# Spreading the tokens' scales: later behind the sums, and as two fp32r passes on split scales in place of fp32

## The chip, the cores and the metric

The kernel runs on one core of one Trainium2 chip. The metric is the device time of one execution in microseconds; a time below is the median of several executions of the same program.

## The reference, cut to what matters

A trunk of four decoder layers works on 256 tokens of 1024 features. A layer is a SwiGLU feed-forward block (hidden size 2816), a token mixer, a second SwiGLU block, and a sigmoid gate on a per-layer embedding. The mixer of layers 0 and 3 is HGRN2, a gated linear recurrence; that of layer 1 is mLSTM; that of layer 2 is attention over a sliding window (SWA). All is float32.

```
h = x + 1/2 * SwiGLU_1(RMSNorm(x))
h = h + Mixer(RMSNorm(h))
h = h + 1/2 * SwiGLU_2(RMSNorm(h))
x = h + sigmoid(RMSNorm(h) W_gate) * (p W_ple)

RMSNorm(x) = x * rsqrt(mean(x*x over the 1024 features) + 1e-6) * gain
```

So there are four RMSNorms in a layer and sixteen in all. Each needs, per token, one sum over the features and one scale made from it.

## The kernel before, in words

**Layout.** The activations lie transposed: features on the 128 partitions, tokens along the row. The four tiles `h[0..3]` hold 1024 features x 256 tokens. All weights stream from memory in 1 MB transfers of two units (a unit is 128 x 1024 numbers). Every float32 operand of the large products is split into two fp32r parts: ScalarE (ACT) casts to the high part (L246), VectorE (DVE) subtracts to get the low part (L247). A product is then three fp32r matmuls, or, in `mm_t`, two: the high weight with both parts of x side by side (512 columns, L278) and the low weight with the high part (256 columns, L279). One such pair is called a tile here. A unit feeds eight tiles, and three units are made ahead of the one in use (`AHEAD_UNITS`).

**The norm.** A product does not wait for the norm's scale: x carries only the gain, and the scale of each token is applied to the result. `end_norm` therefore queues the making of the scale as background work (`later`), and the products tick it along: each tile adds 0.125 to a credit, and when the credit is positive the next step of the first generator in the queue is emitted, and what it yields is taken off. The steps of a norm are four squares (each weighs `W_SQ` = 1.0, eight tiles), then a pause `W_SS`, then the two matmuls with a column of ones (L402), which leave the sums per token on the partitions, the factor and the epsilon on DVE (L376), the power -0.5 on GpSimd (POOL, L377) which gives `rc` (128 tokens x 2), a pause `W_RC` = 0.5 (four tiles), then two matmuls that spread the scales over all partitions (L407: `rc` broadcast as the stationary operand, the identity as the moving one, 128 columns each), and a copy from PSUM on ACT to `rb` (L409). `rc` is used where tokens lie on the partitions, `rb` where features do.

**Who needs them.** In the feed-forward blocks `rb` scales the gates (L428), first when the eighth column tile is done, and later the output (L465). In HGRN2 it scales f and q (L660), and in the PLE gate the products (L520), followed by a sigmoid, two more DVE operations, and the push of the next layer's x (`push`, L250 and L251), which the first tiles of the next layer's feed-forward block read. SWA uses `rc` alone.

**What sets the order.** The code emits in the order told above; the framework then lays the instructions of each engine out itself, by the order in the code and by when it expects the operands to be there, adds the waits, and each engine runs its list strictly in that order. TensorE (PE) is the one on which all norms and products meet.

The constants are made in `setup`, among them `ident` by POOL.

Of the kernel before, what the change touches and what calls it, by code (L numbers as in the profile page):

```python
# [11 lines left out]
F32R = mybir.dt.float32r  # L12
# [6 lines left out]
P = 128  # L19
D = 1024  # L20
T = 256
NT = T // P
# [5 lines left out]
EPS = 1e-6  # L28
U = 1024
AHEAD_UNITS = 3  # L30
W_SQ, W_SS, W_RC = 1.0, 0.5, 0.5
ML_RATE = 1
SW_RATE = 2.5
FQ_RATE = 0.75
# [85 lines left out]
class Kern:  # L120
# [219 lines left out]
    def setup(self):  # L340
        nc, c, a = self.nc, self.const, self.a
        self.h = [c.tile([P, 512], F32, tag=f"h{j}", name=f"h{j}") for j in range(4)]
        self.gains = c.tile([P, DEPTH * N_GAIN * KT], F32, name="gains")
        nc.scalar.dma_start(out=self.gains, in_=a["gains"])
        ncol = a["cols"].shape[1]
        self.cols = c.tile([P, ncol], F32, name="cols")
        nc.scalar.dma_start(out=self.cols, in_=a["cols"])
        self.ident = c.tile([P, P], F32, name="ident")
        make_identity(nc, self.ident)
        self.ones = c.tile([P, 1], F32, name="ones")  # L350
        nc.gpsimd.memset(self.ones, 1.0)
        self.mhalf = c.tile([P, 16], F32, name="mhalf")
        nc.gpsimd.memset(self.mhalf, -0.5)
# [22 lines left out]
        nc.vector.tensor_scalar(out=out, in0=src, scalar1=1.0 / n, scalar2=EPS, op0=ALU.mult, op1=ALU.add)  # L376
        nc.gpsimd.tensor_tensor(out=out, in0=out, in1=self.mhalf[:, :w], op=ALU.pow)  # L377

    def end_norm(self):


        rc = self.small([P, NT], "rc", 2)
        rb = self.small([P, T], "rb", 2)
        return self.x, rc, rb, self.later(self.norm_steps(rc, rb))

    def norm_steps(self, rc, rb):
        nc = self.nc
        ss = self.small([P, T], "ss", 2)
        for j in range(4):
            sq = self.s512("sq")  # L390
            nc.scalar.activation(sq, self.h[j], AF.Square)
            for i in range(2):
                s = sq[:, i * T:(i + 1) * T]
                if i:
                    nc.vector.tensor_tensor(out=ss, in0=ss if j else sq[:, :T], in1=s, op=ALU.add)
                elif j:
                    nc.vector.tensor_tensor(out=ss, in0=ss, in1=s, op=ALU.add)
            yield W_SQ
        yield W_SS
        ps = self.misc()  # L400
        for t in range(NT):
            nc.tensor.matmul(ps[:, t:t + 1], ss[:, t * P:(t + 1) * P], self.ones, start=True, stop=True)  # L402
        self.rsqrt_mean(rc, ps[:, :NT], D, NT)
        yield W_RC
        pb = self.misc()
        for t in range(NT):
            nc.tensor.matmul(pb[:, t * P:(t + 1) * P], rc[:, t:t + 1].broadcast_to([P, P]), self.ident,  # L407
                             start=True, stop=True)
        nc.scalar.copy(out=rb, in_=pb[:, :T])  # L409

    @staticmethod
# [598 lines left out]
    def swa(self, l):  # L1010
        nc = self.nc
        j = l // 3
        x, rc, rb, norm = self.end_norm()
        nc.sync.dma_start(out=self.sinks, in_=self.a["sinks"][j:j + 1, :].broadcast_to([P, SW_H]))
        o = self.col_of["sw_q_norm"] + j
        nc.vector.tensor_scalar(out=self.qg, in0=self.cols[:, o:o + 1], scalar1=SW_D ** -0.5, scalar2=None,
# [239 lines left out]
```

## Time and profile before

| | |
|---|---|
| median of 3 runs | 2122.43 us (2111.08 to 2124.21) |
| the profiled execution | 2116.65 us |
| its span in the trace | 2114.9 us |
| PE busy | 2084.7 us (99%), 12261 matmuls |
| DVE busy | 1540.0 us (73%) |
| ACT busy | 1204.6 us (57%) |
| POOL busy | 52.9 us (2%) |
[...]

The profile is of one execution. Its time is 5.8 us under the median of the three runs and within their spread. Busy shares count an engine's instructions; matmul ends are modelled, so idle gaps of PE are best read from the starts of neighbouring matmuls.

### The profile page before, as it was taken

The page shows a single profiled execution, that of the slowest core. Times are in us where ns is not written, and L with a number is a line of the kernel's source. Part 1 is how long each engine was busy: PE and PEld are TensorE (multiplying, and loading weights), DVE is VectorE, ACT ScalarE, POOL GpSimd, SP SyncE. Part 2 cuts the span into 40 slices and gives each one's busy share as a digit, 9 for nine tenths or more (in the row PEclk, how much of TensorE's full clock was granted, in tenths as well). Part 3 has the DMA queues.
Part 4 walks back from the last instruction along what each step waited for, and adds up shares of the span by engine and source line. Part 5 has one row for each costly group of instructions (what it writes and reads, how often), then busy time and mean ns, then how long its engine had stood idle before and what let it go on. Part 6 is the DMA issues. An engine that isn't in the chain of part 4 may idle for free.

```text
span 2114.9 us, 30560 instructions
## 1 busy us (share of the span) xinstructions
PE 2084.7 (99%) x12261; PEld 1822.4 (86%) x12261; DVE 1540.0 (73%) x2063; ACT 1204.6 (57%) x1678; POOL 52.9 (2%) x84
## 2 busy tenths in 40 slices
PE   8999999999999999999999999999999999999998
PEld 7888889888888888888888887788888888898887
DVE  7766987775877576776687667677687768967766
ACT  7555656554755466655565547655466545565544
POOL 1000000000000000000000001000000000000000
PEclk9999999999999999999999999999999999999999
DMA  7555344555455544555545552355545553445551
GB/s 283 199 187 181 118 160 166 198 191 188 171 190 194 183 160 161 183 182 197 184 176 198 181 198 101 118 182 190 188 169 197 192 191 128 143 177 186 192 187 73
DMA packets 53855, 372.26 MB, mean 176 GB/s; under 512 B 6352, under 2 KB 6992, under 8 KB 9424
## 3 DMA queue, kind: packets, MB, share of 16 engines
q1 hardware_dynamic: 53424, 370.21, 48.5%
q8 instruction: 96, 1.57, 0.3%
q14 instruction: 47, 0.39, 0.1%
q10 hardware_dynamic: 288, 0.09, 0.0%
HBM read 369.23 MB, written 1.05 MB: 175 GB/s over the span
## 4 chain that ended last, share of the span: by engine, by line
PE 91%; DVE 5%; issue 2%; ACT 1%; POOL 1%; DMA 0%; ACTq 0%; DVEq 0%; POOLq 0%
PE acc L278 50%; PE acc L279 26%; PE acc L268 2%; PE acc L260 2%; PE acc L270 2%; PE acc L269 2%; PE acc L259 2%; PE acc L261 2%; PE mis L694 1%; DVE wl L247 1%; DVE slab L701 1%; DVE slab L707 1%; PE mis L1077 1%; POOL rc L377 0%; PE mis L407 0%
## 5 line engine op out<-in xcount | busy, mean ns | idle before, releaser
L278 PE MATMUL acc<-x,wh 128*128 128x512 f32 x3392 | 1188.3, 395 | 8.7 <-DVE x L251 7.2
L247 DVE TENSOR_TENSOR wl<-wraw,wh 128x1024 fp32r<-128x1024 f32 (+1 forms) x693 | 844.5, 1222 | 474.6 <-ACT wh L246 470.6
L246 ACT CAST wh<-wraw 128x1024 fp32r<-128x1024 f32 (+1 forms) x693 | 726.4, 1050 | 750.7 <-PE acc L278 433.4
L279 PE MATMUL acc<-x,wl 128*128 128x256 f32 x3392 | 950.5, 280 | 0.0
L278 PEld LDWEIGHTS acc<-x,wh 128*128 128x128 f32 x3392 | 636.3, 188 | 154.9 <-DVE x L251 8.9
L279 PEld LDWEIGHTS acc<-x,wl 128*128 128x128 f32 x3392 | 640.8, 189 | 0.0
L278 PE MATMUL acc<-slab,wh 128*128 128x512 f32 x1152 | 403.8, 394 | 0.0
L279 PE MATMUL acc<-slab,wl 128*128 128x256 f32 x1152 | 321.9, 279 | 0.0
L278 PEld LDWEIGHTS acc<-slab,wh 128*128 128x128 f32 x1152 | 215.8, 187 | 49.7
L279 PEld LDWEIGHTS acc<-slab,wl 128*128 128x128 f32 x1152 | 217.3, 189 | 0.0
L303 DVE TENSOR_TENSOR gu<-acc,gu 128x512 f32<-128x512 f32 x176 | 120.3, 683 | 6.9 <-ACT gu L302 6.6
L302 ACT COPY gu<-acc 128x512 f32<-128x512 f32 x176 | 101.9, 579 | 14.5 <-PE acc L279 14.5
L268 PE MATMUL acc<-wh,x 128*128 128x512 f32 (+1 forms) x272 | 102.6, 379 | 0.0
L269 PE MATMUL acc<-wl,x 128*128 128x512 f32 (+1 forms) x272 | 100.4, 369 | 0.0
L270 PE MATMUL acc<-wh,x 128*128 128x512 f32 (+1 forms) x272 | 100.1, 368 | 0.0
L278 PE MATMUL acc<-wide,wh 128*128 128x512 f32 x256 | 91.7, 394 | 0.0
L259 PE MATMUL acc<-slab,wh 128*128 128x256 f32 x256 | 74.1, 291 | 0.1
L260 PE MATMUL acc<-slab,wh 128*128 128x256 f32 x256 | 72.9, 285 | 0.0
L261 PE MATMUL acc<-slab,wl 128*128 128x256 f32 x256 | 72.6, 284 | 0.0
L279 PE MATMUL acc<-wide,wl 128*128 128x256 f32 x256 | 71.5, 279 | 0.0
L250 ACT ACTIVATE x<-h,gains 128x256 fp32r<-128x256 f32 x128 | 57.4, 501 | 21.6 <-DVE h L466 19.8
L430 DVE TENSOR_TENSOR gu<-gu,gu 128x512 f32<-128x512 f32 x88 | 60.8, 691 | 5.8 <-ACT gu L429 2.9
(236 smaller groups left out, 1777.0 us busy)
## 6 DMA issues: line engine op xcount, KB each, us to landing
wraw<-in_w_all SPq DMA_DIRECT2D x346, 1024.0 KB, 4.8
wraw<-in_w_all SPq DMA_DIRECT2D x7, 512.0 KB, 8.3
pt<-in_pT SPq DMA_DIRECT2D x4, 256.0 KB, 3.9
h<-in_xT SPq DMA_DIRECT2D x3, 256.0 KB, 5.1
outT<-h SPq DMA_DIRECT2D x3, 256.0 KB, 2.0
wraw<-in_w_all SPq DMA_DIRECT2D x2, 256.0 KB, 4.5
h<-in_xT SPq DMA_DIRECT2D x2, 128.0 KB, 4.4
outT<-h SPq DMA_DIRECT2D x2, 128.0 KB, 1.7
```

Of the source, the lines that this page charges most:

```text
L246: self.nc.scalar.copy(out=hi, in_=src)
L247: self.nc.vector.tensor_tensor(out=lo, in0=src, in1=hi.bitcast(F32), op=ALU.subtract)
L259: mm(ps, wh[:, cs], xh, start=first and opens, stop=False, skip_group_check=True)
L260: mm(ps, wh[:, cs], xl, start=False, stop=False, skip_group_check=True)
L261: mm(ps, wl[:, cs], xh, start=False, stop=last, skip_group_check=True)
L268: mm(ps, xh[:, ts], wh[:, cs], start=first, stop=False, skip_group_check=True)
L269: mm(ps, xh[:, ts], wl[:, cs], start=False, stop=False, skip_group_check=True)
L270: mm(ps, xl[:, ts], wh[:, cs], start=False, stop=last, skip_group_check=True)
L278: mm(ps, wh[:, cs], x, start=first, stop=False, skip_group_check=True)
L279: mm(ps[:, T:], wl[:, cs], x[:, :T], start=False, stop=last, skip_group_check=True)
L302: nc.scalar.copy(out=o3, in_=p4[:, :, 1, :])
L303: nc.vector.tensor_tensor(out=o3, in0=p4[:, :, 0, :], in1=o3, op=ALU.add)
```

## The change

The pause between the sums and the spreading grows from 0.5 to 1.25 (from four tiles to ten), except in SWA, where it stays 0.5. Right after the power, `rc` is split into an fp32r high and low part, as the weights are: a cast on ACT and a subtraction on DVE, 128 x 2 each. The spreading then takes, per half of the tokens, two fp32r matmuls that add up in PSUM, with an fp32r copy of the identity, in place of one fp32 matmul. The copy of the identity is made once at the start, on ACT.

```diff
-W_SQ, W_SS, W_RC = 1.0, 0.5, 0.5
+W_SQ, W_SS, W_RC, W_RC_SW = 1.0, 0.5, 1.25, 0.5
...
         make_identity(nc, self.ident)
+        self.ident_r = c.tile([P, P], F32R, name="ident_r")
+        nc.scalar.copy(out=self.ident_r, in_=self.ident)
...
-    def norm_steps(self, rc, rb):
+    def norm_steps(self, rc, rb, w_rc):
...
         self.rsqrt_mean(rc, ps[:, :NT], D, NT)
-        yield W_RC
+        rh, rl = (self.small([P, NT], n, 2, F32R) for n in ("rch", "rcl"))
+        self.split(rh, rl, rc)
+        yield w_rc
         pb = self.misc()
         for t in range(NT):
-            nc.tensor.matmul(pb[:, t * P:(t + 1) * P], rc[:, t:t + 1].broadcast_to([P, P]), self.ident,
-                             start=True, stop=True)
+            for i, r in enumerate((rh, rl)):
+                nc.tensor.matmul(pb[:, t * P:(t + 1) * P], r[:, t:t + 1].broadcast_to([P, P]), self.ident_r,
+                                 start=i == 0, stop=i == 1)
         nc.scalar.copy(out=rb, in_=pb[:, :T])
...
-        x, rc, rb, norm = self.end_norm()
+        x, rc, rb, norm = self.end_norm(W_RC_SW)
```

## Rows read from the trace of the kernel before

**Rows 1.** The page: busy time by engine (us, share, instructions); the chain by engine.

```profile
PE 2084.7 (99%) x12261; PEld 1822.4 (86%) x12261; DVE 1540.0 (73%) x2063; ACT 1204.6 (57%) x1678; POOL 52.9 (2%) x84
...
PE 91%; DVE 5%; issue 2%; ACT 1%; POOL 1%; DMA 0%; ACTq 0%; DVEq 0%; POOLq 0%
```

**Rows 2.** Waits of PE, then of ACT: total us, times, longest us.

```profile
PE mis L407 <- POOL rc L377: 3.8, 4, 1.1
...
ACT wh L246 <- PE acc L278: 433.4, 319, 3.5
```

**Rows 3.** Line L407 and its SWA case in time (start, us, instruction).

```profile
L407 PE MATMUL mis<-ident,rc x64: 270/275/377, 40.3 to 2099.3; 128*128 128x128 f32 x64
...
1265.57 0.28 PE L269 MATMUL acc<-wl,x 128*128 128x256 f32 x1
1265.69 0.28 PE L270 MATMUL acc<-wh,x 128*128 128x256 f32 x1
1265.81 0.60 PE L407 MATMUL mis<-ident,rc 128*128 128x128 f32 x4
1266.17 0.36 PE L268 MATMUL acc<-wh,x 128*128 128x256 f32 x1
```

**Rows 4.** PE in time around L402 of the same norm.

```profile
1263.83 0.28 PE L270 MATMUL acc<-wh,x 128*128 128x256 f32 x1
...
1264.31 0.36 PE L268 MATMUL acc<-wh,x 128*128 128x256 f32 x1
```

**Rows 5.** PE in time around L407, PLE of layer 0.

```profile
545.99 0.39 PE L278 MATMUL acc<-x,wh 128*128 128x512 f32 x1
...
546.89 0.37 PE L279 MATMUL acc<-x,wl 128*128 128x256 f32 x1
```

**Rows 6.** PE in time around L407, mLSTM norm.

```profile
758.20 0.28 PE L279 MATMUL acc<-x,wl 128*128 128x256 f32 x1
...
759.46 0.48 PE L278 MATMUL acc<-x,wh 128*128 128x512 f32 x1
```

**Rows 7.** PE in time, first norm of layer 1.

```profile
570.05 0.50 PE L402 MATMUL mis<-ones,ss 128*128 128x1 f32 x4
...
571.21 0.27 PE L279 MATMUL acc<-x,wl 128*128 128x256 f32 x1
572.56 0.71 PE L407 MATMUL mis<-ident,rc 128*128 128x128 f32 x4 [1.08 <-POOL rc L377]
573.03 0.48 PE L278 MATMUL acc<-x,wh 128*128 128x512 f32 x1
```

**Rows 8.** Line L278 between 547.05 and 570.04 us, weight loads (ns min/median/max).

```profile
L278 PEld LDWEIGHTS acc<-x,wh x66: 186/187/192, 547.0 to 569.7; 128*128 128x128 f32 x66
```

**Rows 9.** The tile rc: DVE and POOL (ns min/median/max).

```profile
L376 DVE TENSOR_SCALAR rc<-mis x16: 147/151/160, 39.2 to 2097.7; 128x2 f32<-128x2 f32 x16
L377 POOL TENSOR_TENSOR rc<-rc,mhalf x16: 695/698/1608, 39.5 to 2098.0; 128x2 f32<-128x2 f32 x16
```

**Rows 10.** ACT in time at the start.

```profile
4.76 0.62 ACT L246 CAST wh<-wraw 128x512 fp32r<-128x512 f32 x1 [1.75 <-DMA wraw<-in_w_all]
...
8.85 0.21 ACT L600 ACTIVATE lb_e<-lb_e 128x32 f32<-128x32 f32 x1
```

**Rows 11.** HGRN2 of layer 0: DVE and ACT after rb.

```profile
213.19 1.22 DVE L660 TENSOR_TENSOR slab<-slab,rb 128x1024 f32<-128x1024 f32 x1
...
215.97 1.28 ACT L661 ACT_TABLE_LOAD   x1
```

**Rows 12.** PLE of layer 0: ACT's rb, DVE's first push.

```profile
547.17 0.37 ACT L409 COPY rb<-mis 128x256 f32<-128x256 f32 x1 [0.36 <-PE mis L407]
...
553.58 0.88 DVE L251 SCALAR_TENSOR_TENSOR x<-h,gains,x 128x256 fp32r<-128x256 f32 x2 [0.36 <-ACT x L250]
```

**Rows 13.** The end: DVE on the last column tile.

```profile
2109.87 0.42 DVE L303 TENSOR_TENSOR gs<-acc,gs 128x256 f32<-128x256 f32 x1 [1.30 <-ACT gs L302]
```

**Rows 14.** ACT in time, SWA norm: what waits for POOL.

```profile
1265.52 0.84 ACT L999 ACTIVATE sq<-acc,rc 128x256 f32<-128x256 f32 x2 [2.43 <-POOL rc L377]
```

More of the change, by code (lines that the diff above doesn't have):

```diff
@@ L377, in rsqrt_mean, with end_norm @@
         nc.gpsimd.tensor_tensor(out=out, in0=out, in1=self.mhalf[:, :w], op=ALU.pow)
-    def end_norm(self):
+    def end_norm(self, w_rc=W_RC):
         rc = self.small([P, NT], "rc", 2)
         rb = self.small([P, T], "rb", 2)
-        return self.x, rc, rb, self.later(self.norm_steps(rc, rb))
-    def norm_steps(self, rc, rb):
+        return self.x, rc, rb, self.later(self.norm_steps(rc, rb, w_rc))
+    def norm_steps(self, rc, rb, w_rc):
         nc = self.nc
```

## The prediction, made before the result was known

> **What bounds the kernel.** I read the page first: PE is busy 99% of the span and the chain that ended last runs on PE for 91% [rows 1]. The time is therefore the sum of what PE executes plus the few places where it stands, and anything on DVE, ACT or POOL counts only where PE waits for it. The list of PE's waits comes next. The scale's power on POOL is named there for 3.8 us in 4 waits [rows 2]; a wait is counted only from the modelled end of the matmul before, so I read the true price from start to start, in PE's timeline around each of the sixteen L407 groups.
>
> **What a norm's spreading costs PE now.** In SWA the group waits for nothing. From L270 to the next L268 it is 0.48 us, where undisturbed neighbours lie 0.12 apart: the four passes of the two fp32 products insert 0.36 us [rows 3]. That is the bare price; the last PLE (0.37) and the first block (0.45) repeat it. Elsewhere a wait comes on top. Between L278 and its L279, normally 0.23 apart, lie 0.90 us in PLE 0: 0.67 inserted [rows 5]; the other two such PLEs cost the same, and the two HGRN2 norms and four second feed-forward norms 0.55 to 0.60 (3.46 together). The mLSTM norm costs 1.26 - 0.12 = 1.14 [rows 6]. The first norms of layers 1 to 3 cost 1.82 - 0.12 = 1.70 each, 5.12 together [rows 7]. Sum: 1.18 + 3 x 0.67 + 3.46 + 1.14 + 5.12 = 12.9 us, of which 16 x 0.37 = 5.9 is the bare insertion and 7.0 is waiting for `rc`. So 7.0 us, 0.33% of the time, is all that a later place can return.
>
> **Part 1, the later place.** Six tiles more are 6 x 0.35 = 2.1 us of other PE work, where `rc` now comes 0.1 to 0.8 us late. In the eleven norms where the wait is 0.8 or less it goes: 7.0 - 3 x 1.34 = 3.0 us. The three first norms of layers 1 to 3 are different. There L402 already runs late, because the squares of the last pushed h come late: after PLE 0's L407, which lies in tile 42 of 64, PE starts 66 tiles before L402 [rows 8], so L402 stands behind tile 44, not behind tile 37 where its step falls due. L407 follows only two and a half tiles on [rows 7], fewer than the four of the old pause. Its place is set by when the framework expects the scale, and a due time of tile 47 changes that place by half a tile at most. The real delay is POOL's: its power takes 0.70 us at the median and 1.61 in four cases, these three and mLSTM [rows 9]. I count nothing for these three; if all of it went, it would be 4.0 us more. **-3.0 us, bounds -7.0 and 0.**
>
> **Part 2, the passes.** Four passes stay four: an fp32 product is two passes now (64 records for 32 products), and an fp32r product pair is two. No row shows an fp32r pass of 128 columns. From below: fp32r passes of 256 columns start 0.12 apart [rows 3]; half of that is 0.058, four are 0.23, 0.13 less than now, 2.1 us in sixteen norms. From above: an fp32r pass could take what a whole fp32 product of 128 columns takes, twice 0.108 (L407's four passes span 0.60, each lasts 0.275 [rows 3]); four are 0.86, 0.50 more, 8.0 us. I take no change, because the nearest row says that columns do not set the price: L402, with one moving column, inserts the same 0.36 us as L407 with 128 [rows 4], so what is left is the weight load of each pass, and there are still four (an fp32r load lasts 187 ns [rows 8]). **0, bounds -2.1 and +8.0.**
>
> [...]
>
> **Part 3, the split.** Per norm one ACT cast, at most the 0.21 us of a 128x32 operation [rows 10], and one DVE subtraction like L376, 0.15 us [rows 9]; 16 x 0.36 us off PE's path, under the six tiles of cover. SWA keeps the old pause, and its L407 came just as `rc` was there: +0.4 us. In the three uncovered norms the scale is later by 0.36 too, but the framework can move the place with it: 0 (bounds 0 and 3 x 1.6, if the subtraction also stands behind a 1.2 us weight subtraction). The copy of the identity falls into ACT's 1.75 us of waiting for the first weights [rows 10]: 0; uncovered it would be about 0.3 us. **+0.4 us, up to +5.2.**
>
> **Part 4, a later `rb`.** No DMA moves. `rb` lands about 1.6 us later (from the middle of tile 42 to behind tile 47). The gates of the feed-forward blocks need it at tile 64, so nothing there. Three places are close. HGRN2: L660 ends at 214.41 and ACT's next step begins at 215.97 [rows 11], 1.56 us of slack for 1.6 of delay; behind it is a chain that PE does wait for. I take 0.3 for each of the two layers, at most 1.6 each. PLE into the next layer: the first half of the first push ends at about 554.0 [rows 12] and PE asks for it at 546.89 + 22.5 x 0.35 = 554.7, so 0.7 us of slack; of the 6.5 us from `rb` to that push about 1.9 are other work that can go first. I take 0.4 us for each of three layers, at most 1.3 each. The end: DVE stood 1.30 us before the last column tile [rows 13], against 2.1 us of delay there: +0.4, at most 0.8. **+2.2 us, bounds 0 and +7.9.**
>
> **Sum.** -3.0 + 0 + 0.4 + 2.2 = -0.4 us. On the profiled execution of 2116.65 us this is 2116.2; that execution lies 5.8 us under the median of 2122.43, on which it would be 2122. The four executions shown average 2118.6, so I forecast **2118 us: no difference that a measurement can tell** (about 1% is the least that it can for this kernel).
>
> **Rivals.**
> - *The waits of layers 1 to 3 go too* (22%). The due time then does decide there. For it: the new due tile is 47, the place now is 46 to 47. Against: L407 is spaced by readiness. Another -4.0: 2114; with part 4 hidden, 2112.
> - *The passes cost their columns only* (8%): -2.1, 2116. Against it stands L402's row.
> - *An fp32r pass of 128 columns costs as much as an fp32 product* (18%). Its place is L407 itself; +8.0, so 2126, slower than before. It decides as soon as a pass inserts 0.1 us, since the net gain is only 0.4 us. For it: no row shows a fast one this narrow. Against: the columns do not set the price now.
> - *The queues stand* (4%). The cast waits on ACT for POOL, the subtraction on DVE for the cast, and behind them stand the weights' casts and subtractions; PE waits for the weights. That such a wait holds the rest is in the trace: ACT stood 2.43 us at L999 for `rc` [rows 14]. Price: POOL's 14.8 us plus 16 x 0.36 = 20.6 us if nothing covers it, 2139, and 2159 with a 1.2 us subtraction in front each time. It decides where fewer than about 2 us of weights lie ahead. Against: ACT's casts wait 433 us for PE to free a buffer [rows 2], so weights are ready ahead nearly everywhere.
> - *The change does not move L407* (6%): the framework keeps it where the scale is expected. 2118 to 2119.
>
> [...]
>
> **Chances.** The forecast has 42%. Every case but the queues lies between 2112 and 2126. The runs of before lie 7.5 us under and 5.6 over their mean, so I widen to 2107 to 2129. Over 1% faster (under 2101) would need more than all waits and all insertions together, 12.9 us: 2%, for scatter alone. Over 1% slower (over 2143) is most of the queue case: 4%. Within 1%: 94%.
>
> **What would show it.** Right: no PE wait for POOL at L407 outside the first norms of layers 1 to 3, where a wait of about 1 us stays, now for DVE's low part; an insertion near 0.37 us in the other norms; L407's place behind ten tiles after L402; small new waits of PE for x (L251) at the start of layers 1 to 3. Wrong: passes starting 0.06 or 0.2 us apart; waits for `wl` on PE; the three waits of layers 1 to 3 gone.

## The result: 1% slower

| | before | after |
|---|---|---|
| median (4 runs each) | 2118.86 us (2111.08 to 2124.21) | 2145.32 us (2132.91 to 2148.14) |
| ratio, 95% interval | | 1.0105 (1.0081 to 1.0129) |
| profiled execution, span | 2114.9 us | 2143.6 us |

The forecast was 2118 us, the range 2107 to 2129: the time lies outside it, on the slower side. Nothing in the changed kernel's totals says why. The page's busy times and its chain by engine are nearly those of [rows 1]:

```profile
PE 2108.2 (98%) x12261; PEld 1836.1 (86%) x12261; DVE 1543.0 (72%) x2079; ACT 1208.2 (56%) x1695; POOL 51.9 (2%) x84
...
PE 92%; DVE 5%; ACT 1%; issue 1%; POOL 0%; DMA 0%; SPq 0%; DVEq 0%; ACTq 0%; POOLq 0%
```

PE's number of instructions is the same, and it is busy 23.5 us longer: much of the loss is no wait at all, but the same matmuls taking longer. The waits of PE, answering to [rows 2], give the other part (total us, times, longest us):

```profile
PE acc L278 <- DVE x L251: 16.2, 4, 7.7
PE mis L699 <- DVE slab L706: 4.0, 4, 1.1
PE acc L278 <- DVE gs L303: 3.4, 1, 3.4
PE mis L1054 <- ACT kd L1045: 2.5, 1, 2.5
```

The waits for `rc` are gone. In their place PE waits for the pushed x: one of the four is the start (7.2 us before, 7.7 here), the other three are 2.8 us each, at the first tile of layers 1, 2 and 3. The wait for `gs` at the end was 1.4 us before.

**The spreading itself.** In SWA, answering to [rows 3] (PE in time):

```profile
1274.94 0.28 PE L270 MATMUL acc<-wh,x 128*128 128x256 f32 x1
1275.06 0.28 PE L412 MATMUL mis<-ident_r,rch 128*128 128x128 f32 x1
1275.20 0.33 PE L412 MATMUL mis<-ident_r,rcl 128*128 128x128 f32 x1
1275.37 0.27 PE L412 MATMUL mis<-ident_r,rch 128*128 128x128 f32 x1
...
1275.59 0.33 PE L268 MATMUL acc<-wh,x 128*128 128x256 f32 x1
```

From L270 to L268 it is 0.65 us, so 0.53 inserted where the fp32 passes inserted 0.36. The first norm of layer 1, answering to [rows 7]:

```profile
577.29 0.28 PE L279 MATMUL acc<-x,wl 128*128 128x256 f32 x1
577.41 0.22 PE L412 MATMUL mis<-ident_r,rch 128*128 128x128 f32 x1
577.47 0.28 PE L412 MATMUL mis<-ident_r,rcl 128*128 128x128 f32 x1
...
577.80 0.45 PE L278 MATMUL acc<-x,wh 128*128 128x512 f32 x1
```

From L279 to L278 it is 0.51 us: 0.51 - 0.12 = 0.39 inserted, against 1.70 before. The first two passes start 0.06 us apart here. Over the sixteen norms the insertion fell from 12.9 to 7.4 us. The tile `rc` and the split, answering to [rows 9] (ns min/median/max):

```profile
L378 DVE TENSOR_SCALAR rc<-mis x16: 149/150/161, 41.1 to 2123.0; 128x2 f32<-128x2 f32 x16
L379 POOL TENSOR_TENSOR rc<-rc,mhalf x16: 697/698/1544, 41.3 to 2123.3; 128x2 f32<-128x2 f32 x16
L246 ACT CAST rch<-rc x16: 185/190/193, 42.0 to 2124.1; 128x2 fp32r<-128x2 f32 x16
L247 DVE TENSOR_TENSOR rcl<-rc,rch x16: 152/155/163, 42.3 to 2124.3; 128x2 fp32r<-128x2 f32 x16
```

**The PLE of layer 0.** ACT from `rb` on, then DVE, answering to [rows 12]:

```profile
550.15 0.37 ACT L414 COPY rb<-mis 128x256 f32<-128x256 f32 x1 [1.88 <-PE mis L412]
550.49 1.05 ACT L246 CAST wh<-wraw 128x1024 fp32r<-128x1024 f32 x1
551.44 0.58 ACT L302 COPY gs<-acc 128x512 f32<-128x512 f32 x1
552.04 1.28 ACT L526 ACT_TABLE_LOAD   x1
```

```profile
550.56 1.29 DVE L525 TENSOR_TENSOR gs<-gs,rb 128x512 f32<-128x512 f32 x2 [1.05 <-ACT rb L414]
551.77 1.22 DVE L247 TENSOR_TENSOR wl<-wraw,wh 128x1024 fp32r<-128x1024 f32 x1
552.90 0.68 DVE L303 TENSOR_TENSOR gs<-acc,gs 128x512 f32<-128x512 f32 x1
553.62 0.69 DVE L525 TENSOR_TENSOR gs<-gs,rb 128x512 f32<-128x512 f32 x1
554.23 1.28 DVE L527 TENSOR_TENSOR gs<-gs,pw 128x512 f32<-128x512 f32 x2
555.44 1.28 DVE L528 TENSOR_TENSOR h<-gs,h 128x512 f32<-128x512 f32 x2
...
558.38 1.66 DVE L251 SCALAR_TENSOR_TENSOR x<-h,gains,x 128x256 fp32r<-128x256 f32 x4
```

Before, ACT loaded the sigmoid's table directly behind `rb` (at 547.56, 1.28 us long), and DVE took the first two products (L522) and sums one tile after the other. Now a weight's cast and the next column tile's copy come ahead of the table, and on DVE the first two tiles go side by side: their gates, a weight's subtraction, both products, both sums, the third tile's product, another weight's subtraction, and only then their pushes. From the start of `rb` to the first push it was 6.41 us and is 8.23. PE then, and the windows around it (start:end, length; busy us and instructions of PE, its weight loads, DVE, ACT and POOL; then the granted clock, 1.00 being full speed (on the mean of the span it is 1.000 before and 0.992 here); then the DMA share and GB/s):

```profile
555.88 0.28 PE L279 MATMUL acc<-x,wl 128*128 128x256 f32 x1
559.00 0.47 PE L278 MATMUL acc<-x,wh 128*128 128x512 f32 x1 [2.84 <-DVE x L251]
...
560.92 0.63 PE L278 MATMUL acc<-x,wh 128*128 128x512 f32 x1
561.35 0.41 PE L279 MATMUL acc<-x,wl 128*128 128x256 f32 x1
561.56 0.63 PE L278 MATMUL acc<-x,wh 128*128 128x512 f32 x1
```

```profile
550.00:555.50 5.50, 5.50 (x33) 4.79 (x32) 4.91 (x8) 5.32 (x8) 0.00 (x0) 1.00 0.33 97
560.00:563.00 3.00, 3.00 (x11) 2.54 (x10) 3.00 (x8) 1.74 (x4) 0.00 (x0) 0.50 0.00 0
```

The wait is followed by about five tiles at 0.64 us in place of 0.35: the granted clock is 0.50. That is 1.5 us more, so each of the three waits costs about 4.3 us in this execution. The end repeats it. DVE takes three tiles' products and two sums ahead of a fold that frees PSUM for PE, and its stand before the last column tile, 1.30 us in [rows 13], is 2.84. PE in time:

```profile
2133.53 0.79 PE L278 MATMUL acc<-x,wh 128*128 128x512 f32 x1 [3.38 <-DVE gs L303]
2134.12 0.41 PE L279 MATMUL acc<-x,wl 128*128 128x256 f32 x1
2134.33 0.63 PE L278 MATMUL acc<-x,wh 128*128 128x512 f32 x1
```

That is 2.0 us more of waiting than before and four tiles at half clock (0.50 from 2134 to 2136 us), 1.2 us.

**The tiles.** The last part shows only in counts. These are the matmuls of L278 alone in 160 us of the first layer's second feed-forward block (window, length, busy us and count of the matmuls, then of their weight loads, then clock and DMA), in the kernel before and then in a second execution of the changed kernel (e6 below).

```profile
380.00:540.00 160.00, 160.00 (x463) 86.56 (x462) 1.00 0.53 190
```

```profile
380.00:540.00 160.00, 160.00 (x454) 85.12 (x453) 1.00 0.52 186
```

160 us / 463 is 346 ns a tile, 160 / 454 is 352 (the tiles cut at the window's ends count as whole), at full clock in both and with no wait between. In every profile the long stretches, from one norm to the next, run at one of two spacings, 347 or 353 ns from tile to tile. A slow stretch of a second feed-forward block (some 500 tiles) costs 3 us.

**The account** of 28.7 us between the two spans: three waits for x 8.5; tiles at half clock 6.4 (22 more); the start's wait 0.5; the end's 2.0; SWA 6.4, nearly all of it a lower clock in this execution (0.76 and 0.83 in two windows of 20 us; 0.8 us in the second execution); the mean tile 350.8 in place of 348.4 ns over 4,700 tiles 11.2; the spreading -5.5. Sum 29.5, 0.8 too many.

### The profile page after: what moved, and what is told of

It reads as the page before. It is cut to its first block, busy times and chain, and to the rows that moved or that the text cites. A ratio compares the mean times of both kernels' runs of the same rounds, so it can differ in the third digit from the quotient of the medians.

```text
span 2143.6 us, 30618 instructions
## 1 busy us (share of the span) xinstructions
PE 2108.2 (98%) x12261; PEld 1836.1 (86%) x12261; DVE 1543.0 (72%) x2079; ACT 1208.2 (56%) x1695; POOL 51.9 (2%) x84
## 4 chain that ended last, share of the span: by engine, by line
PE 92%; DVE 5%; ACT 1%; issue 1%; POOL 0%; DMA 0%; SPq 0%; DVEq 0%; ACTq 0%; POOLq 0%
PE acc L278 51%; PE acc L279 26%; PE acc L268 2%; PE acc L270 2%; PE acc L269 2%; PE acc L260 2%; PE acc L261 2%; PE acc L259 2%; PE mis L699 1%; DVE wl L247 1%; PE mis L1082 1%; DVE slab L706 1%; DVE slab L712 1%; PE mis L687 0%; DVE gs L527 0%
## 5 line engine op out<-in xcount | busy, mean ns | idle before, releaser
L278 PE MATMUL acc<-x,wh 128*128 128x512 f32 x3392 | 1203.7, 399 | 19.7 <-DVE x L251 16.2
L279 PE MATMUL acc<-x,wl 128*128 128x256 f32 x3392 | 953.7, 281 | 0.0
L278 PEld LDWEIGHTS acc<-x,wh 128*128 128x128 f32 x3392 | 641.2, 189 | 174.3 <-issue 9.4
L279 PEld LDWEIGHTS acc<-x,wl 128*128 128x128 f32 x3392 | 644.3, 190 | 0.0
L278 PE MATMUL acc<-slab,wh 128*128 128x512 f32 x1152 | 406.7, 396 | 0.0
L279 PE MATMUL acc<-slab,wl 128*128 128x256 f32 x1152 | 322.3, 280 | 0.0
L278 PEld LDWEIGHTS acc<-slab,wh 128*128 128x128 f32 x1152 | 216.2, 188 | 52.1
L279 PEld LDWEIGHTS acc<-slab,wl 128*128 128x128 f32 x1152 | 217.3, 189 | 0.0
L268 PE MATMUL acc<-wh,x 128*128 128x512 f32 (+1 forms) x272 | 103.4, 383 | 0.0
L270 PE MATMUL acc<-wh,x 128*128 128x512 f32 (+1 forms) x272 | 101.2, 372 | 0.0
L278 PE MATMUL acc<-wide,wh 128*128 128x512 f32 x256 | 92.4, 396 | 0.0
L279 PE MATMUL acc<-wide,wl 128*128 128x256 f32 x256 | 71.6, 280 | 0.0
L433 DVE TENSOR_TENSOR gu<-gu,rb 128x512 f32<-128x512 f32 x88 | 60.7, 692 | 8.0 <-ACT rb L414 5.4
```

What stands on the lines that cost most here:

```text
L268: mm(ps, xh[:, ts], wh[:, cs], start=first, stop=False, skip_group_check=True)
L270: mm(ps, xl[:, ts], wh[:, cs], start=False, stop=last, skip_group_check=True)
L278: mm(ps, wh[:, cs], x, start=first, stop=False, skip_group_check=True)
L279: mm(ps[:, T:], wl[:, cs], x[:, :T], start=False, stop=last, skip_group_check=True)
```

## The experiments

Ratios are to the kernel before on the same chip, with their 95% interval. "Stretches" are the four behind the spreadings of the second feed-forward blocks.

**e1, the pause alone.** `W_RC` 1.25 (SWA 0.5), the rest as before.

> Kernel before with the longer pause alone (fp32 passes, no split; SWA keeps 0.5). Theory A (the later rb in the PLE norms makes the next layer's first x late; PE stands 2.8 us three times and 3.4 us at the end, and its clock falls to half for about 3 us after each): those four waits are here too, 12 us and 6 to 7 us of half clock, less the 6 to 7 us of waits for rc that go: 2128 to 2133 against 2119 for before. Theory B (the split and the fp32r passes cost the time): none of the four waits, 2112 to 2114.

1.0033 (1.0019 to 1.0048). The three waits are there (2.9 us each), without split or fp32r passes, but the ratio is a third of the loss: theory A explains the waits and not the time.

**e2, the split with the old pause.** The changed kernel with `W_RC` = 0.5.

> Changed kernel with the old pause of 0.5 everywhere (split and fp32r passes alone). Theory A: the four waits for x and gs are gone; the waits for the scale at the spreading grow by about 0.4 us per norm; SWA's wait for kd and its half clock (6 to 8 us in the changed kernel) may stay: 2122 to 2132. Theory B: as slow as the changed kernel, 2140 to 2146.

1.0069 (1.0057 to 1.0081), and the three waits of 2.8 us are there too: here `rb` is late because the low part stands behind a weight's subtraction on DVE. So not the pause, but a later `rb` by any cause brings the wait.

**e3, the old pause in the PLE alone.** In `ple`: `self.end_norm(W_RC_SW)`.

> Changed kernel with the pause of 0.5 in the PLE norms as well as in SWA. Theory A: the four waits and the half clock behind them go, 17 to 19 us: 2124 to 2130, the rest being SWA's. Theory B: 2140 to 2146.

1.0077 (1.0062 to 1.0092); the waits stay, for the reason of e2; the wait at the end falls to 1.4 us.

**e4, the longer pause outside the PLE.** e1 with 0.5 in `ple` too.

> Kernel before with the longer pause alone, and that neither in the PLE norms nor in SWA. Theory A: no new wait, and the waits for rc in the first norms of layers 1 to 3, the mLSTM norm and the small ones outside PLE go, 5 to 6 us: 2112 to 2115. Theory B: also 2112 to 2114; this run is the version that should beat both if A holds.

0.9995 (0.9985 to 1.0005). No wait for x. With e1 this puts the PLE's later `rb` at 0.0038, 8 us. But the waits for `rc` went outside the first norms and the PLE, and the time did not fall. The tiles' spacing may have taken it back: of the eight long stretches behind the feed-forward norms four ran at 353 ns in its profile, against two in the first profile of the kernel before and three in e5. One execution each does not show it.

**e5 and e6, both kernels again.** No edit.

> The kernel before, unchanged. In the first profile the tiles of the feed-forward blocks run at 347 or at 353 ns, a block at a time. If that is a state of the single execution (theory A), another execution has the slow spacing in other blocks and its span differs by 3 us for each block, 2114.9 +- 8 us, with no new wait. If it is set by the program (rival), the same blocks are slow again and the span is within 1 us of 2114.9.

> The changed kernel, unchanged. By both theories PE waits again 2.8 us for x at the start of layers 1 to 3 and 3.4 us for gs at the end, since the program fixes those. Open is SWA: if its lower granted clock (0.76 from 1280 to 1300 us, 0.83 from 1340 to 1360) belongs to the program, it is there again within 0.05; if it is a chance of the execution, one of the two stretches is at 0.95 or more and the span is 3 us or more under 2143.6.

e5: span 2119.1 us, the same waits; the stretch behind the last layer's first norm at 353 ns where it had 347: the spacing is not fixed by the program alone. But the four stretches had 347 again. e6: span 2142.7, the waits as they were, SWA's clock at 1.00 and 0.91 in the two windows that had 0.76 and 0.83, and SWA, from its sums to those of the next norm, 107.1 us long as against 112.7 (106.3 before); four of four stretches at 353. Most of SWA's loss was thus of that execution; the total did not fall, since more tiles were slow. (The profile of e2 has SWA at 112.9 us again.)

**e7, the split in SWA alone.**

> The kernel before, with the split and the two fp32r passes in the SWA norm alone, all pauses as before. Theory A: in SWA the split has no cover (the spreading came just as the scale was there), what follows is late and PE's clock falls there, as in the changed kernel: 2125 to 2128 us, clock under 0.9 in a stretch between 1260 and 1360 us. Rival: the split costs its own 0.4 us and SWA's loss came from what lay ahead of it: 2119 to 2121 us, clock 0.97 or more there. No wait for x at the start of a layer by either.

1.0010 (0.9998 to 1.0021): by its time theory A falls. The lowest clock, 0.91 from 1320 to 1340 us, lies between what the two expected. SWA is 0.8 us longer than before, but that is not shown to be the split's price: e14 and e18 below, without the split in SWA, have one such stretch of lower clock there too and the same length, 107.0 us. All eight profiles with the split in SWA have such a stretch and five of the twelve without, so whether the split invites it stays open.

**e8, the PLE first.** The changed kernel, in `flush` of `ple`:

```diff
-                add(j, gs, 0, 2)
-                if not last:
-                    self.push(j)
+                with self.tc.high_priority():
+                    add(j, gs, 0, 2)
+                    if not last:
+                        self.push(j)
```

> The changed kernel, with the PLE's gates and the push of x behind them put ahead in the framework's order (ACT then takes the sigmoids before the copy of the next column tile, DVE the products and sums before the third tile's and a weight's subtraction). rb is as late as in the changed kernel. Theory A (the wait of 2.8 us is the order that the later rb brings, not rb's lateness itself): the waits for x shrink from 2.8 to about 0.9 us each, the clock stays above 0.95 at the starts of layers 1 to 3, and the time is 7 to 10 us under the changed kernel's 2145: 2135 to 2138. Rival (rb's lateness itself): the waits stay at 2.5 us or more and the time at 2142 to 2147.

1.0072 (1.0052 to 1.0091), 2129.99 us: by ratio 7 us under the changed kernel, though the two intervals overlap. PE's wait at the start of layer 1, then DVE from `rb` to the push:

```profile
560.35 0.47 PE L278 MATMUL acc<-x,wh 128*128 128x512 f32 x1 [0.99 <-DVE x L251]
```

```profile
553.75 1.29 DVE L525 TENSOR_TENSOR gs<-gs,rb 128x512 f32<-128x512 f32 x2 [1.05 <-ACT rb L414]
...
559.74 0.47 DVE L251 SCALAR_TENSOR_TENSOR x<-h,gains,x 128x256 fp32r<-128x256 f32 x1
```

The wait is 1.0 us, with 1.00 as the clock behind it. `rb` (553.35) to the push is 6.39 us, as before the change: theory A holds for the waits. The sum closes: `rb` comes 7.5 us ahead of the tile that needs x before (554.7 less 547.17) and 5.85 ahead after (556.0 less 550.15), 1.7 less; the order adds 8.23 - 6.41 = 1.8; the slack was 0.7. 1.7 + 1.8 - 0.7 = 2.8, and 1.0 without the order's part.

**e9, the longer pause in the second feed-forward norms alone.** fp32 passes; `self.end_norm(W_RC_F1 if f else W_RC)`.

> The kernel before, with the longer pause in the norms of the four second feed-forward blocks alone; fp32 passes. Their four spreadings stop waiting (0.55 to 0.60 us inserted now, 0.37 then): 0.8 us less. Theory A (a short wait of PE at the spreading leaves the tiles behind it at 347 ns, none leaves them at 347 or 353): one to three of the four stretches behind these spreadings run at 353 ns in the profile, where none of twelve did in three profiles with the old pause; each costs about 3 us up to the PLE's norm, so 2 to 9 us more: 2 to 8 us over the kernel before. Rival (the spacing has nothing to do with the place): all four at 347 ns or no more slow ones than elsewhere, and the time 1 us under to 1 us over the kernel before.

1.0014 (1.0002 to 1.0026); one stretch of four at 353. A weak yes: its sign is that of theory A, and its size is hardly above the scatter.

**e10, the split and fp32r passes outside the PLE and SWA.** e4 with them.

> The changed kernel, with fp32 passes and the old pause in the PLE and SWA norms: e4 with the split and the two fp32r passes added in the other eleven norms. PLE keeps the order of the kernel before, so no wait of 2.8 us for x by either theory. Theory A (the split and the fp32r passes cost something of their own beyond the PLE, through the tiles' spacing behind the spreading): 5 to 9 us over the kernel before, at least two of the four stretches of the second feed-forward blocks at 353 ns. Rival (outside the PLE they are free): as e4, within 2 us of the kernel before.

1.0075 (1.0061 to 1.0089), more than either theory had. No wait for x, clock 0.999, and four of four stretches at 353: against e4 the difference is 0.0080, 17 us. By this pair three quarters of the loss are here, with no new wait for x to show for it.

**e11, the pause alone with the PLE first.** e1 with e8's edit.

> e1 (longer pause, fp32 passes, no split) with the PLE's gates and push put ahead in the framework's order, as in e8. Theory A (order): the three waits for x shrink from 2.8 to 0.5 us or less (rb is about 0.4 us earlier than in e8, where 1.0 was left), the clock stays full there, and 4 to 8 us of e1's 7 over the kernel before go: -1 to +3 us. The 3.3 us wait for gs at the end stays. Rival (rb's lateness itself): waits of 2 us or more stay, +5 to +8 us.

1.0039 (1.0025 to 1.0053): the waits for x shrink from 2.9 to 1.0 us and the clock stays at 1.00 there, but by ratio the time does not fall under e1's (theory A had it 4 to 8 us under). In the first norms of layers 1 to 3 PE waits for `rc` again (2.5 us in 3), and the end's wait is 3.9. The order's part is shown by the waits; what it is worth in time, this pair does not show.

**e12, the old pause in the second feed-forward norms.** The changed kernel, `self.end_norm(W_RC_SW if f else W_RC)`.

> The changed kernel, with the old pause in the norms of the four second feed-forward blocks. Theory A (the wait sets the spacing): PE waits there again for the scale's parts, 0.2 to 1 us each, and the four stretches behind run at 347 ns (in the two profiles of the changed kernel seven of eight ran at 353): 4 to 10 us under the changed kernel, 2135 to 2141 us. Rival: the waits come back and nothing else changes: 1 to 4 us over the changed kernel, 2146 to 2149. The three waits of 2.8 us for x stay by both.

(The expectation counted the slow ones wrongly: six of eight.) 1.0088 (1.0072 to 1.0103), 2133.33 us: all four stretches at 347 ns, as theory A has it. By ratio that is 0.0017, 4 us, under the changed kernel, with overlapping intervals. The three waits of 2.8 us stay.

**The place in the tile.** In these traces one thing goes with the spacing. With the old pause the spreading lies inside a tile, between L278 and its L279; with the long one mostly between two tiles. (In e2 and e12 PE takes the four fp32r passes of these norms in two places: one pass inside a tile, the other three inside a later one, behind the low part.) PE in time at the same norm (layer 1, second block), in the kernel before and then in the changed kernel:

```profile
872.43 0.40 PE L278 MATMUL acc<-x,wh 128*128 128x512 f32 x1
872.75 0.71 PE L407 MATMUL mis<-ident,rc 128*128 128x128 f32 x4
873.22 0.36 PE L279 MATMUL acc<-x,wl 128*128 128x256 f32 x1
```

```profile
877.40 0.28 PE L279 MATMUL acc<-x,wl 128*128 128x256 f32 x1
877.52 0.22 PE L412 MATMUL mis<-ident_r,rch 128*128 128x128 f32 x1
...
877.98 0.45 PE L278 MATMUL acc<-x,wh 128*128 128x512 f32 x1
```

The next four kernels tick all background work inside the tile:

```diff
         mm(ps, wh[:, cs], x, start=first, stop=False, skip_group_check=True)
+        self.tick(mid)
         mm(ps[:, T:], wl[:, cs], x[:, :T], start=False, stop=last, skip_group_check=True)
...
-            self.tick(0.125)
```

**e13, the kernel before so; e14, e4 so.**

> The kernel before, with every background step ticked between the two matmuls of a tile instead of behind the second one. Theory A (the place in the tile sets the spacing behind it): fifteen spreadings, where they fall inside a tile, leave 347 ns; the two to four stretches that run at 353 in the kernel before mostly go to 347, each 0.5 to 3 us: 1 to 6 us under the kernel before. Rival (place and spacing only go together by chance): mean spacing and time as before, within 2 us.

> e4 (longer pause outside PLE and SWA, fp32 passes) with every background step ticked inside the tile. Theory A: all four stretches of the second feed-forward blocks and both HGRN2 stretches at 347 ns (e4: one and two of them at 353): 3 to 8 us under e4's ratio of 0.9995, so 0.996 to 0.998. Rival: as e4.

e13: 0.9998 (0.9989 to 1.0006), all four at 347 as before; nothing to gain there. e14: 0.9982 (0.9973 to 0.9990), all four and both HGRN2 stretches at 347: with fp32 passes a place inside the tile goes with the fast spacing throughout (the table below), and the longer pause then returns a little.

**e15, the changed kernel so; e16, e10 so.**

> The changed kernel with every background step ticked inside the tile. Theory A: the stretches behind its spreadings go from 353 to 347 ns, 8 to 14 us under the changed kernel (ratio to before 1.004 to 1.008); the three waits of 2.8 us for x stay. Rival (the split or the passes slow the tiles wherever they lie): at least half of the stretches stay at 353 and the ratio at 1.010 or more.

> e10 (split and longer pause outside PLE and SWA) with every background step ticked inside the tile. Theory A: e10's ratio of 1.0075 falls to 1.000 +- 0.002, its four stretches of the second feed-forward blocks go from 353 to 347 ns; with e15 this closes the account: what is left of the loss is the PLE's order. Rival: 1.005 or more.

e15: 1.0112 (1.0095 to 1.0130), four of four at 353: the rival. e16: 1.0037 (1.0024 to 1.0051), two of four: between the two. So the place does not decide for fp32r passes. Behind the first norms of layers 1 to 3 of e15, whose four passes lie inside a tile too but insert 0.39 us and not 0.64, all three stretches ran at 347.

**e17, the four passes two and two.** e16 with `yield 0.125` between the halves.

> e16 with the spreading's four fp32r passes dealt over two neighbouring tiles, two inside each. Theory A (four in one place leave the slow spacing, two and two do not): the four stretches of the second feed-forward blocks and the two of HGRN2 at 347 ns, ratio 0.998 to 1.001 to the kernel before. Rival (fp32r passes leave it as chance has it, wherever they lie): one or more of the four at 353, ratio 1.003 or more.

1.0095 (1.0077 to 1.0112), four of four at 353: theory A falls. The extra step also puts off HGRN2's (PE waits 8.4 us for a slab there, 4.3 in e16).

**e18, the split made but not used.** e16 with fp32 passes on `rc`.

> e16 with the split made and not used: the spreading takes the fp32 passes on the unsplit scale. Theory A (the fp32r passes are what costs): as e14, ratio 0.997 to 0.999, stretches at 347 ns. Rival (the split's cast and subtraction are what costs): as e16, 1.003 or more.

0.9976 (0.9966 to 0.9986), 2110.39 us: theory A holds, and it is, with e14, the version that beats both kernels. The pair e18 and e16 differs in the passes alone (and so in what they wait for: `rc` or its parts). The first stretch's count and the spreading in PE's time, first of e18, then of e16:

```profile
380.00:540.00 160.00, 160.00 (x463) 86.32 (x462) 1.00 0.52 190
```

```profile
363.29 0.39 PE L278 MATMUL acc<-x,wh 128*128 128x512 f32 x1
363.51 0.61 PE L414 MATMUL mis<-ident,rc 128*128 128x128 f32 x4
363.88 0.36 PE L280 MATMUL acc<-x,wl 128*128 128x256 f32 x1
```

```profile
380.00:540.00 160.00, 160.00 (x454) 85.06 (x454) 1.00 0.51 185
```

```profile
364.82 0.39 PE L278 MATMUL acc<-x,wh 128*128 128x512 f32 x1
365.05 0.22 PE L414 MATMUL mis<-ident_r,rch 128*128 128x128 f32 x1
...
365.58 0.27 PE L414 MATMUL mis<-ident_r,rcl 128*128 128x128 f32 x1
365.69 0.33 PE L280 MATMUL acc<-x,wl 128*128 128x256 f32 x1
```

From L278 to its partner 0.59 us with fp32, 0.87 with fp32r. Between the two spans (2108.8 and 2121.1) lie 12.3 us: 2.3 in the insertions and some 10 in the tiles' mean spacing (347.7 and 349.9 ns, 4,700 tiles).

| passes and place, second feed-forward norms | kernels | stretches at 353 ns |
|---|---|---|
| fp32, inside a tile | before, e5, e7, e13, e14, e18 | 0 of 24 |
| fp32, between tiles | e1, e4, e9, e11 | 5 of 16 |
| fp32r, between tiles | after, e6, e3, e8, e10 | 14 of 20 |
| fp32r, four inside one tile | e15, e16 | 6 of 8 |
| fp32r, one inside a tile, three in a later one | e2, e12 | 0 of 8 |
| fp32r, two and two in neighbouring tiles | e17 | 4 of 4 |

The stretches behind the first norms of layers 1 to 3 in the same profiles bear the first three rows out: fp32 inside a tile 0 of 9, fp32 between tiles 8 of 21, fp32r between tiles 10 of 12. With fp32r inside they are mixed: 2 of 6 with four in one tile, 6 of 12 with one and three. So one and three is no safe place either; only behind fp32 passes inside a tile was the slow spacing never found.

## Why the prediction was wrong

By ratios, the change is the sum of: the pause outside the PLE and SWA -0.0005 (e4), the later `rb` in the PLE +0.0038 (e1 less e4), the fp32r passes +0.006 to +0.008 (e16 less e18, e10 less e4). Together 0.009 to 0.011; measured 0.0105. That this closes so well is in part luck: the parts were measured in different surroundings, and the middle one is unsure. After less e10 and e15 less e16, which both hold the PLE and SWA, give 0.0030 and 0.0075, and e11, with most of the wait gone, was no faster than e1.

- **Part 1, the waits: right in kind, larger.** -5.5 us at the spreadings against -3.0. The three first norms fell from 1.70 to 0.39, which the prediction left out and gave to a rival (22%). That rival's reason, the due time, is not borne out: without the 2.8 us wait for x (e4, e8, e10, e11) PE still waits 0.7 to 0.9 us there; with it and the long pause (after, e6, e1, e3, e12, e15) it does not. So it was most likely the new wait that gave POOL its time. And the returned time bought nothing by itself: e4 lost 3.1 us of waiting at the spreadings (12.9 to 9.8 inserted) and gained nothing.
- **Part 2, the passes: the step that failed most.** The prediction set them at 0 because four passes stay four; that the weight load of each is the price was its estimate, and no run shows it (a load's record lasts 185 to 192 ns, while the passes start 0.06 to 0.16 us apart in fifteen of the sixteen groups). The last two of each group do start 0.11 us apart, like fp32's, but the whole is not the same: 0.39 to 0.53 us inserted between tiles against 0.36, and 0.64 inside (e16). (Where 0.39 is inserted, the first two passes are 0.06 apart, which the prediction had named as a sign that it is wrong.) That is some 2 us. What the prediction had no term for is what the passes leave behind them: 353 in place of 347 ns for hundreds of tiles, 10 us. The rival "as dear as an fp32 product" had the sign and, by its +8.0, about the size, with another mechanism: it looked at L407 alone.
- **Part 3, the split: right, and smaller still.** 0.19 and 0.16 us an operation; in SWA no price of its own is shown where +0.4 was set (e7 is as long there as e14 and e18), and nothing elsewhere (e18 against e14). Only in the PLE, with the old pause, does the low part behind a 1.2 us subtraction make `rb` late (e2, e3): the prediction had that delay, but at the three first norms.
- **Part 4, the later `rb`: failed in the PLE.** The delay was foreseen (1.6 us, measured 1.7) and so was the slack (0.7). What failed is "of the 6.5 us about 1.9 are other work that can go first": the framework put more ahead, not less, and the way from `rb` to x grew by 1.8. So 2.8 us each in place of 0.4, over the bound of 1.3, and 1.5 at half clock on top, for which no term stood (e8, with the order put back, has waits of 1.0 us and the clock at 1.00). The end was mis-sized the same way: 2.0 of wait and 1.2 of clock against 0.4. HGRN2 lost nothing (its waits on L699 are 4.0 us, on L694 in e5 4.6).
- **The queues** did not stand: ACT's casts wait 9.6 us for the power on POOL, and PE never for weights. The range was too narrow because it took a cost only where an instruction is added or a wait appears.

What stays open: why fp32r passes leave the slow spacing more often than fp32 ones, why at the second feed-forward norms two and two left it behind four times of four and one and three never, and what the two spacings are.

## What to carry to other kernels

A step that is moved in the code is laid out anew by the framework: compare the order of instructions on each engine, not only the step's own time, and ask what stands between the moved result and the first matmul that needs it. PE was busy 98% of the changed kernel's span, and 11.2 us of its loss was the tiles' mean spacing, with no wait: count matmuls in equal windows before and after. A wait of PE can be dearer than it looks: here 2.84 us of it cost about 4.3, as the granted clock stood at 0.50 behind it.

## What the runs showed of the hardware

- The same pair of matmuls (512 and 256 columns) has two spacings at a granted clock of 1.00, 347 and 353 ns (463 and 454 of L278 in 160 us), and held one over hundreds of tiles, from one norm to the next: in the kernel before 347 from 400 to 540 us and, two spreadings on, 353 from 580 to 640. In a slow stretch the tiles take 350, 350 and 360 ns in turn (the first norm of layer 1 in the kernel before), in a fast one 346 or 347 each (e18, 400 to 540 us) or 343 and 350 in turn (the kernel before, 400 to 540 us).
- After a wait of 2.84 us the granted clock was 0.50 for about five tiles, beginning 0.5 to 0.9 us after PE had started again (the three waits of the changed kernel). Over seven profiles (after, e1, e2, e3, e6, e12, e15) it fell at 17 of the 21 waits of 2.7 to 2.9 us for x; after the six waits of 1.0 us in e8 and e11 it stayed at 1.00.
- Of the four fp32r passes of 128 columns in a spreading (L412 of the changed kernel, sixteen groups) the last two start 0.11 us apart throughout. The second and third start 0.11 apart in five groups, where the first two are 0.06 apart (577.41 and 577.47, and then up to 577.80), and 0.16 apart in ten, where the first two are 0.08 to 0.15 apart; in the first block's group the starts are 0.33, 0.06 and 0.11 apart. The last three passes of fp32 (L407 of the kernel before) start 0.11 apart in all sixteen groups. The record of a weight load of the fp32r passes lasts 185 to 192 ns.
